# Two MLPs in a written instruction order instead of the scheduler's, on one core

## The chip, the cores and the metric

The kernel runs on one core of one Trainium2 chip. The metric is the device time of one execution, in microseconds (us). The engines are named as in the profile: PE (TensorE, matrix products), PEld (its weight loads), DVE (VectorE), ACT (ScalarE), POOL (GpSimd) and SP (SyncE, which here only issues DMAs). Each engine takes its instructions from a queue of its own, and semaphores hold an instruction until what it needs is there.

## The reference

Two layers on 256 tokens of width 2048 in float32: stick-breaking attention, then an MLP; native sparse attention (NSA), then an MLP. What the change touches is the MLP, once in each layer:

```python
def sqrelu_mlp(h, w1, w2):
    return jnp.square(jax.nn.relu(h @ w1)) @ w2
# D_MODEL = 2048, SEQ = 256, D_FF = 8192
    h = h + sqrelu_mlp(rms_norm(h, mlp_norm_g[layer]), mlp_w1[layer], mlp_w2[layer])
```

## The kernel before

**Numbers as pairs.** Every float32 operand of a product is split into two parts of a faster format, `hi` and `lo`: ACT copies it to `hi` (L142), and DVE subtracts to get `lo` (L144). A product is then three: hi by hi, lo by hi, hi by lo. The residual stream `h` stays in SBUF; `xhi`/`xlo` (tile `xs`) is the normalized and transposed input of the next projection, `yhi`/`ylo` the hidden values of an MLP.

**Chunks.** Weights arrive in chunks of 256 x 512 (512 KB), one DMA on SP each (`load`, L157), into one of five `raw` buffers; inside an MLP every sixth load goes to a buffer of its own, `raw6`. A chunk is split into one of four `hi` and four `lo` buffers and then multiplied. There are three kinds: a T chunk (`chunk_T`, L206, 24 matmuls with the weights stationary) for `x @ w1`; an N chunk (`chunk_N`, L173, 12 matmuls of 512 columns) for `y @ w2`; and an S chunk (`chunk_S`, L269), which does the same as an N chunk with 21 matmuls of 256 columns, seven products instead of eight, at the price of more work on ACT (`shi`) and DVE (`ts`, `slo`).

**The MLP.** The hidden width is done in four groups `fg` of 2048. `group1` makes 2048 hidden values in four blocks of eight T chunks; after each block ACT takes the relu, the square and `yhi`, DVE `ylo` and the sums for the S chunks (L447 to L460). `group2` multiplies them by `w2` in four column blocks: blocks 0 and 1 as N chunks, block 2 as S chunks between them (`in_S`), block 3 as S chunks between the T chunks of the next group. `add_h` and `add_S` add a finished block to `h`. In the last group of a layer block 3 is done as N chunks, and `done` is called for each block: in the first MLP it starts the next layer's input, in the second it stores the block with a DMA on SP (L1090).

**Seams.** `out_proj` ends each attention and adds its last block to `h` (L384). The input of the following MLP is made by `next_x`: two sums of squares on ACT (`junk`, L349), then for each pair of 128 columns four transposes on PE (L328), two evacuations on ACT (`xs`, L333) and two on DVE (L335). These steps lie in a list, `beside`, and `pump` takes a step from it after the two halves of each chunk.

**The order.** The code issues instructions in program order, but outside the first projection, which is written under `manual_schedule`, a scheduler reorders each engine's list by its own estimates. It may therefore put the split of a later chunk ahead of a step that waits. Memory of the pool `small`, which holds `junk`, lies ahead of the weight buffers.

## Time and profile before

| | us |
|---|---|
| median of 3 runs | 2145.69 (2145.44 to 2146.96) |
| profiled execution, its own time | 2144.79 |
| its span, first to last instruction | 2143.1 |
| first MLP, roughly | 392 to 1074 of the span |
| second MLP, roughly | 1459 to 2141 of the span |

Times in the trace are microseconds from the start of the span. A row of the order in time reads: start, duration, engine, line, operation, output tile <- input tile, shape, count, and in brackets the idle time before it and what ended it. A row by stretch gives, for each engine, busy time and number of instructions, then the granted clock of PE, the share of the DMA engines and GB/s. A matmul's duration in the trace includes a modelled end, so the distance from one start to the next is the better measure of it.

### The profile page before, as it was taken

How to read it: one execution, taken by the hardware profiler on the slowest of the kernel's cores; microseconds unless marked ns; L12 is line 12 of the kernel's file. 1: busy time of each engine (PE TensorE's matmuls, PEld its weight loads, DVE VectorE, ACT ScalarE, POOL GpSimd, SP SyncE). 2: the span in 40 equal slices, each digit the busy share in tenths (PEclk: the TensorE clock that was granted, in tenths of full speed). 3: DMA queues.
4: the chain of work that ended last, by engine and by line, in shares of the span. 5: the costliest groups of instructions: out<-in, count | busy, mean ns of one | idle time of the engine just before them, and what ended most of it. 6: DMA issues, size and time to landing. Idle time of an engine off the chain costs nothing.

```text
span 2143.1 us, 37272 instructions
## 1 busy us (share of the span) xinstructions
PE 2136.4 (100%) x14894; PEld 1973.4 (92%) x14894; DVE 1563.9 (73%) x2131; ACT 1231.6 (57%) x1653; POOL 45.2 (2%) x75
## 2 busy tenths in 40 slices
PE   9999999999999999999999999999999999999999
PEld 9999988998998999999898888889989989989998
DVE  5556556567878778778777888765678797788786
ACT  6555665555555555565555666655655555655653
POOL 0000000000000000000000111000000000000000
PEclk9999999999999999999999999999999999999999
DMA  7655556665665666665667654456656656656664
GB/s 240 210 172 177 158 180 186 186 195 188 207 202 186 205 197 203 217 197 186 194 185 217 169 145 136 149 177 187 197 170 215 205 188 213 197 189 210 204 195 149
DMA packets 260789, 406.34 MB, mean 190 GB/s; under 512 B 13188, under 2 KB 91912, under 8 KB 260616
## 3 DMA queue, kind: packets, MB, share of 16 engines
q1 hardware_dynamic: 259800, 403.52, 60.2%
q8 instruction: 116, 1.90, 0.4%
q10 hardware_dynamic: 816, 0.46, 0.1%
q14 instruction: 57, 0.47, 0.1%
HBM read 401.83 MB, written 2.10 MB: 188 GB/s over the span
## 4 chain that ended last, share of the span: by engine, by line
PE 98%; DVE 1%; DMA 0%; ACT 0%; issue 0%; POOL 0%; SPq 0%; DVEq 0%; ACTq 0%; POOLq 0%
PE acc L206 43%; PE acc L173 37%; PE att L269 12%; PE att L173 1%; PE att L328 1%; PE att L944 1%; DMA raw<-in_nsa_w_in_dram 0%; DVE lo L144 0%; PE att L655 0%; PE att L607 0%; PE att L882 0%; PE att L938 0%; PE att L884 0%; PE att L883 0%; PE att L936 0%; PE att L937 0%
## 5 line engine op out<-in xcount | busy, mean ns | idle before, releaser
L142 ACT ACTIVATE hi<-raw 128x1024 fp32r<-128x1024 f32 x639 | 676.0, 1060 | 576.1 <-PE acc L206 274.0
L144 DVE TENSOR_TENSOR lo<-raw,hi 128x1024 fp32r<-128x1024 f32 x639 | 776.6, 1222 | 252.9 <-ACT hi L142 241.3
L206 PE MATMUL acc<-xs,hi 128*128 128x256 f32 x5360 | 665.2, 277 | 0.0
L206 PEld LDWEIGHTS acc<-xs,hi 128*128 128x128 f32 x5360 | 634.4, 188 | 0.9
L206 PE MATMUL acc<-xs,lo 128*128 128x256 f32 x2680 | 359.3, 277 | 0.0
L206 PEld LDWEIGHTS acc<-xs,lo 128*128 128x128 f32 x2680 | 329.2, 188 | 0.0
L173 PE MATMUL acc<-hi,yhi 128*128 128x512 f32 x828 | 324.9, 393 | 0.0
L173 PE MATMUL acc<-hi,ylo 128*128 128x512 f32 x828 | 323.4, 391 | 0.0
L173 PE MATMUL acc<-lo,yhi 128*128 128x512 f32 x828 | 224.3, 392 | 0.0
L245 DVE TENSOR_TENSOR ts<-raw 128x512 f32<-128x512 f32 x112 | 77.4, 691 | 167.2 <-DMA raw<-in_mlp_w_dram 166.7
L142 ACT ACTIVATE hi<-ts 128x1024 fp32r<-128x1024 f32 x112 | 118.7, 1060 | 136.8 <-PE acc L173 67.8
L173 PEld LDWEIGHTS acc<-lo,yhi 128*128 128x128 f32 x828 | 154.7, 188 | 31.6
L173 PEld LDWEIGHTS acc<-hi,ylo 128*128 128x128 f32 x828 | 155.7, 188 | 29.5 <-DVE ylo L315 0.2
L173 PEld LDWEIGHTS acc<-hi,yhi 128*128 128x128 f32 x828 | 155.6, 188 | 29.5 <-ACT yhi L314 0.2
L173 PE MATMUL acc<-hi,xs 128*128 128x512 f32 x704 | 177.2, 392 | 0.0
L173 PEld LDWEIGHTS acc<-hi,xs 128*128 128x128 f32 x704 | 130.3, 188 | 26.1
L144 DVE TENSOR_TENSOR lo<-ts,hi 128x1024 fp32r<-128x1024 f32 x112 | 136.5, 1219 | 3.5 <-ACT hi L142 3.5
L247 ACT ACTIVATE shi<-raw 128x768 fp32r<-128x768 f32 x112 | 94.6, 845 | 54.8 <-PE att L269 34.5
L250 DVE TENSOR_TENSOR slo<-raw,shi 128x768 fp32r<-128x768 f32 x112 | 106.7, 953 | 4.8 <-PE att L269 4.8
L173 PE MATMUL acc<-lo,xs 128*128 128x512 f32 x352 | 97.1, 396 | 0.0
L269 PE MATMUL att<-hi,ss 128*128 128x256 f32 x672 | 94.4, 276 | 0.0
L269 PEld LDWEIGHTS att<-hi,ss 128*128 128x128 f32 x672 | 84.5, 188 | 0.0
(248 smaller groups left out, 2119.7 us busy)
## 6 DMA issues: line engine op xcount, KB each, us to landing
raw<-in_mlp_w_dram SPq DMA_DIRECT2D x512, 512.0 KB, 4.3
raw<-in_sb_w_qkv_dram SPq DMA_DIRECT2D x95, 512.0 KB, 3.9
raw<-in_nsa_w_in_dram SPq DMA_DIRECT2D x50, 512.0 KB, 3.8
raw<-in_sb_w_out_dram SPq DMA_DIRECT2D x32, 512.0 KB, 3.9
raw<-in_nsa_w_in_dram SPq DMA_DIRECT2D x64, 256.0 KB, 3.8
raw<-in_nsa_w_out_dram SPq DMA_DIRECT2D x32, 512.0 KB, 3.6
w1t<-in_nsa_cmp_w_dram SPq DMA_DIRECT2D x8, 512.0 KB, 4.0
h<-in_x_dram SPq DMA_DIRECT2D x8, 256.0 KB, 4.5
```

Of the source, the lines that this page charges most:

```text
L142: nc.scalar.activation(hi, raw, AF.Copy)
L144: nc.vector.tensor_tensor(lo, raw, hi.bitcast(F32), op=OP.subtract)
L173: mm = lambda a, b, k, t, s, e: nc.tensor.matmul(ps[t], a[:, k, t * P:(t + 1) * P], b, start=s, stop=e)
L206: nc.tensor.matmul(o, w, x[:, k0 + kk, :], start=s, stop=e, skip_group_check=True)
L245: nc.vector.tensor_tensor(ts[:, :2, :], flat[:, W:3 * W].rearrange("p (a n) -> p a n", a=2), b12, op=OP.subtract)
L247: nc.scalar.activation(hi, flat[:, :3 * W], AF.Copy)
L250: nc.vector.tensor_tensor(lo, flat[:, :3 * W], hi.bitcast(F32), op=OP.subtract)
L269: nc.tensor.matmul(ps[i], a, w, start=s, stop=e, skip_group_check=True)
L328: nc.tensor.transpose(ps[:, j * T + t * P:j * T + (t + 1) * P], h[:, t, (kp + j) * P:(kp + j + 1) * P], ident)
L944: nc.tensor.transpose(ptp[:w, j * P:(j + 1) * P], src(j), ident)
```

## The change

The MLP is issued under `manual_schedule`: PE, DVE, ACT and SP take its instructions in the order of the code. The order is written as a plan, a list of chunks with the other steps put behind chosen chunks. The evaluation of a block of hidden values is cut into four steps (relu and square; `yhi` and the sums; one half of the sums' split and `ylo`; the other half), which stand behind the third to sixth chunk that follows the block. The square is taken in place, so the tile `pre` goes; the temporary `uv` of `add_S` moves to the tile `sums`. Three extra raw buffers `more` replace `raw6`: eight in all. `junk` has one buffer instead of two. The output blocks of the second MLP are stored by a DMA on POOL's queue. Instructions keep their work; all lines after L37 move by at least one.

```diff
-        if sixth is not None and loads % 6 == 0:
-            raw = sixth.tile([P, nk, nn], F32, name="raw6", bufs=1)
+        if more is not None and loads % 8 in (2, 5, 7):
+            raw = more.tile([P, nk, nn], F32, tag="more", name="more", bufs=3)
...
-            j = small.tile([P, NB], F32, tag="junk", name="junk")
+            j = small.tile([P, NB], F32, tag="junk", name="junk", bufs=JUNK)
...
+        def relu(fb):
+            a = part["s", fb] = junk.tile([P, KB, T], F32, tag="sq", name="sq", bufs=1)
+            for j in range(0, KB, 2):
+                nc.scalar.activation(
+                    a[:, j:j + 2, :], banks["T", fb][j // 2].rearrange("p (m t) -> p m t", m=2), AF.Relu
+                )
+        def square(fb):
+            s = part["s", fb]
+            nc.scalar.activation(s, s, AF.Square)
...
+            def stages(after, j, fb):
+                put(after, j, do(relu, fb), do(square, fb))
+                for i, f in enumerate((high, low, low7)):
+                    put(after, j + 1 + i, do(f, fb))
+
+            for fg in range(NG):
+                after = {}
+                plain = sum([Ts(fg, fb) for fb in range(NF)], [])
+                if fg:
+                    put(after, 1, do(sum7, 2))
+                    put(after, 3, do(sum2, 1))
+                    Ss(fg - 1, 3, (3, 5, 10, 13, 18, 21, 26, 29), after)
+                for fb in range(NF - 1):
+                    stages(after, fb * NK + NK + 2, fb)
+                yield from merge(plain, after)
+                after = {}
+                if fg:
+                    put(after, 1, do(sum7, 3))
+                stages(after, 2, NF - 1)
+                if fg < NG - 1:
+                    plain = Ns(fg, 0) + Ns(fg, 1)
+                    Ss(fg, 2, (4, 6, 7, 9, 10, 11, 13, 14), after)
+                    put(after, 11, do(sum2, 0))
+                else:
+                    plain = Ns(fg, 0) + Ns(fg, 1) + Ns(fg, 3)
+                    put(after, 10, do(sum2, 0))
+                    Ss(fg, 2, (4, 6, 8, 10, 11, 13, 15, 17), after)
+                    put(after, 17, do(sum2, 1))
+                    put(after, 18, do(sum7, 2), *[do(done, n, (att, "att")) for n in range(3)])
+                    if last is None:
+                        put(after, 23, do(sum2, 3), do(done, 3, (att, "att")))
+                yield from merge(plain, after)
...
+        with tc.manual_schedule(engines={mybir.EngineType.PE, mybir.EngineType.DVE, mybir.EngineType.Activation,
+                                         mybir.EngineType.SP}):
+            steps = list(plan())
+            for n, c in enumerate(steps):
+                if callable(c):
+                    c()
+                    continue
...
-                nc.sync.dma_start(ov[:, :, nb * NB:(nb + 1) * NB], h[:, :, nb * NB:(nb + 1) * NB])
+                nc.gpsimd.dma_start(ov[:, :, nb * NB:(nb + 1) * NB], h[:, :, nb * NB:(nb + 1) * NB])
```

`merge` yields the chunks of `plain` in turn and after each what `after` holds for its index; `sum7` is `add_S`, `sum2` is `add_h`; `chunk1`, `chunk7` and `chunk2` call `chunk_T`, `chunk_S` and `chunk_N`.

The order on ACT at the seam into the second MLP, before: `hi` rows are splits of chunks, and the four ahead of the junk rows are those of the first four T chunks.

```order
L142 ACTIVATE hi<-raw 128x1024 x3
L142 ACTIVATE hi<-raw_15576 128x1024
L142 ACTIVATE hi<-raw 128x1024
L349 ACTIVATE junk,ssq<-h 128x512 x2
L142 ACTIVATE hi<-raw 128x1024 x2
L333 ACTIVATE xs<-att,gT 128x256 x2
L142 ACTIVATE hi<-raw 128x1024
L333 ACTIVATE xs<-att,gT 128x256 x2
```

The same place after; here the `hi<-more` row ahead of the junk rows is the split of the first T chunk, which was loaded into a `more` buffer.

```order
L143 ACTIVATE hi<-raw 128x1024
L143 ACTIVATE hi<-more 128x1024
L350 ACTIVATE junk,ssq<-h 128x512 x2
L143 ACTIVATE hi<-raw 128x1024
L334 ACTIVATE xs<-att,gT 128x256 x2
L143 ACTIVATE hi<-raw 128x1024
L334 ACTIVATE xs<-att,gT 128x256 x2
L143 ACTIVATE hi<-more 128x1024
```

The squares and the two pairs of evacuations moved three places toward the front among the splits: one split stands ahead of the squares where there were four. PE's rows there are the same in both, with the transposes after the second and the third T chunk.

The end of the first MLP on DVE, before: `lo` rows are splits of N chunks, `uv` and the `h` rows (L298) are `add_S` of the last S block, and the `lo` rows right ahead of it are of the three N chunks behind that block.

```order
L144 TENSOR_TENSOR lo<-raw_11312,hi 128x1024
L144 TENSOR_TENSOR lo<-raw,hi 128x1024 x2
L298 SCALAR_TENSOR_TENSOR h<-att,factor,h 128x512
L144 TENSOR_TENSOR lo<-raw,hi 128x1024
L294 TENSOR_TENSOR uv<-att,uv 128x256
L295 TENSOR_TENSOR uv<-att,uv 128x256
L296 TENSOR_TENSOR uv<-att,uv 128x256
L298 SCALAR_TENSOR_TENSOR h<-att,factor,h 128x512
L298 SCALAR_TENSOR_TENSOR h<-uv,factor,h 128x512 x2
L144 TENSOR_TENSOR lo<-raw,hi 128x1024 x2
```

The same place after: the one `lo<-more` row is of the only N chunk that is split between the S block and `add_S`.

```order
L145 TENSOR_TENSOR lo<-more,hi 128x1024
L295 TENSOR_TENSOR uv<-att,uv 128x256
L296 TENSOR_TENSOR uv<-att,uv 128x256
L297 TENSOR_TENSOR uv<-att,uv 128x256
L299 SCALAR_TENSOR_TENSOR h<-att,factor,h 128x512 x2
L299 SCALAR_TENSOR_TENSOR h<-uv,factor,h 128x512 x2
L145 TENSOR_TENSOR lo<-raw,hi 128x1024 x2
L336 SCALAR_TENSOR_TENSOR xs<-att,gT,xs 128x256 x4
```

The whole of `add_S` moved ahead of two or three splits. On ACT at that place, the squares and the evacuations for the next layer's input stand, before, behind the splits of chunks that PE reaches later:

```order
L142 ACTIVATE hi<-raw 128x1024 x3
L293 ACTIVATE uv<-att 128x256
L142 ACTIVATE hi<-raw 128x1024
L349 ACTIVATE junk,ssq<-h 128x512
L142 ACTIVATE hi<-raw 128x1024
L333 ACTIVATE xs<-att,gT 128x256 x4
L349 ACTIVATE junk,ssq<-h 128x512
L142 ACTIVATE hi<-raw 128x1024 x2
L333 ACTIVATE xs<-att,gT 128x256 x4
```

After, each group of evacuations stands right behind the split of the chunk around whose `lo` matmuls PE makes the transposes:

```order
L143 ACTIVATE hi<-more 128x1024
L294 ACTIVATE uv<-att 128x256
L143 ACTIVATE hi<-raw 128x1024
L350 ACTIVATE junk,ssq<-h 128x512 x2
L143 ACTIVATE hi<-raw 128x1024
L334 ACTIVATE xs<-att,gT 128x256 x4
L143 ACTIVATE hi<-more 128x1024
L350 ACTIVATE junk,ssq<-h 128x512 x2
L143 ACTIVATE hi<-raw 128x1024
L334 ACTIVATE xs<-att,gT 128x256 x4
L143 ACTIVATE hi<-more 128x1024
```

So an evacuation moved from a place four splits later to the place right behind the split of its own chunk; on PE the first two of the three pairs of transposes in the MLP's last chunks stand one N chunk later, and the third pair follows the second at once.

## The prediction

> **What bounds the kernel now.** I read the page's engine table first, then the busy time by stretch (cut at the borders of the two MLPs), then who waits for whom on TensorE, then the order in time at the places where the new order differs.

> ```profile
> span 2143.1 us, 37272 instructions
> PE 2136.4 (100%) x14894; PEld 1973.4 (92%) x14894; DVE 1563.9 (73%) x2131; ACT 1231.6 (57%) x1653; POOL 45.2 (2%) x75
> PE 98%; DVE 1%; DMA 0%; ACT 0%; issue 0%; POOL 0%; SPq 0%; DVEq 0%; ACTq 0%; POOLq 0%
> ```
> ```profile
> 391.00:1060.00 669.00, 669.00 (x5074) 636.00 (x5073) 520.81 (x647) 381.08 (x413) 0.70 (x1) 1.00 0.62 198
> 1090.00:1458.80 368.80, 367.78 (x1931) 308.93 (x1930) 275.13 (x537) 226.95 (x483) 24.30 (x18) 1.00 0.58 168
> 1473.00:2120.00 647.00, 647.00 (x4906) 615.30 (x4905) 504.51 (x622) 366.36 (x387) 0.00 (x0) 1.00 0.63 199
> 2120.00:2143.10 23.10, 19.12 (x101) 16.28 (x99) 10.30 (x15) 3.97 (x5) 0.00 (x0) 1.00 0.16 57
> ```
> ```profile
> PE att L515 <- POOL ident masks.py:199: 1.6, 1, 1.6
> PE att L789 <- DVE hs L784: 0.5, 1, 0.5
> ```

> TensorE is the bound, at clock 1.00, and in both MLPs it has no idle time: 669.00 of 669.00 and 647.00 of 647.00. Its waits of a whole run are led by 1.6 us, at the very start. So there is nothing in the MLPs that a better order could save: the change can only keep TensorE fed as well, or worse. The profiled execution took 2144.8 (span 2143.1 and 1.7 around it); the median of the runs is 0.9 above it.

> **The change, part by part.** TensorE's own list stays the same matmuls; in six groups one S chunk stands one T chunk later, which costs nothing while no operand is late.

> *Square in place, four steps.* The same four ACT and six DVE instructions per block; only their places move. Over the first MLP ACT is busy 381 of 669 us and DVE 521, both in the shadow of TensorE, so their durations cost 0 as long as splits keep ahead. In the steady groups they do: relu is placed after the third chunk of the next block and waits for the last of the old one, so three split chunks, of 2.8 us each (below), stand ready for TensorE. 0.

> *8 raw buffers.* Loads run further ahead, past DVE's waits for weights:

> ```profile
> DVE ts L245 <- DMA raw<-in_mlp_w_dram: 166.7, 81, 4.2
> ```

> That is much, but it is DVE's idle time, and TensorE waited for none of it. Gain 0; no loss either, DMA is busy 0.63.

> *The written order at the seam into each MLP.* This is where I see the price. Into the second MLP the trace of before runs like this:

> ```profile
> 1458.14 1.06 ACT L142 ACTIVATE hi<-raw 128x1024 fp32r<-128x1024 f32 x1 [1.61 <-PE acc L173]
> 1458.85 2.05 PE L206 MATMUL acc<-xs,hi 128*128 128x256 f32 x16
> 1459.54 0.63 ACT L349 ACTIVATE junk<-h 128x512 f32<-128x512 f32 x1 [0.34 <-DVE h L384]
> ...
> 1460.98 1.06 ACT L142 ACTIVATE hi<-raw 128x1024 fp32r<-128x1024 f32 x1
> ...
> 1461.67 2.05 PE L206 MATMUL acc<-xs,hi 128*128 128x256 f32 x16
> ...
> 1464.50 0.60 PE L328 MATMUL att<-ident,h 128*128 128x128 f32 x4
> 1464.85 2.07 PE L206 MATMUL acc<-xs,hi 128*128 128x256 f32 x16
> ...
> 1465.14 0.84 ACT L333 ACTIVATE xs<-att,gT 128x256 fp32r<-128x256 f32 x2 [0.27 <-PE att L328]
> ```

> A T chunk lasts 2.82 (1458.85 to 1461.67). At 1458.85 ACT has split the first four chunks; the `hi` at 1460.98 is already that of the fifth. So the squares (junk), which wait for the last block of `h`, and the evacuations (xs), which wait for transposes, delay splits that are not urgent. In the new order ACT has one split, then the two squares, then the second split, xs, the third split, xs, the fourth. Nothing is in hand. TensorE's order is unchanged, so:
> - Second chunk: its `hi` can't start before 1460.98, ends 1462.04, and TensorE wants it at 1461.67: with 0.1 for the handover 0.5 late.
> - Third chunk: the transposes ahead of it start at 1464.50 and are followed 0.35 later by the chunk. Now that chunk's `hi` stands behind xs on ACT: 0.64 until xs starts, 0.84 for the two, 1.06 for `hi`, less 0.35: 2.2 late. Handover (0.1) and the 0.1 by which ACT's instructions overlap cancel.
> - Fourth chunk: the same, 2.2. After it ACT has no more of these and needs 1.06 per 2.82: it recovers.

> The sum is 4.9 per seam. The seam into the first MLP has the same rows, so twice: 9.8. DVE's `lo` (1.2) follows each `hi` and is needed only after sixteen matmuls (1.88, 1464.85 to 1466.73): covered. The page of before has this very chain once, in its first stage, where the order is also written out: transposes, xs, `hi` behind xs, and TensorE waits:

> ```profile
> 5.68 0.84 ACT L333 ACTIVATE xs<-att,gT 128x256 fp32r<-128x256 f32 x2 [2.59 <-PE att L328]
> 6.41 1.17 ACT L527 ACTIVATE hi<-raw 128x512 fp32r<-128x512 f32 x2
> 7.09 0.41 PE L534 MATMUL acc<-xs,hi 128*128 128x256 f32 x1 [0.17 <-ACT hi L527]
> ```

> There the first half `hi` (0.6) lets TensorE start 1.41 after xs began; a full one makes it 1.9, and 0.64 + 1.9 - 0.35 is again 2.2. [...]

> *The end of an MLP.* Here the sums of the last S block (uv, then four times h, on DVE) come one N chunk after that block, where before three splits were in hand:

> ```profile
> 2122.44 0.28 PE L269 MATMUL att<-lo,yhi 128*128 128x256 f32 x1
> ...
> 2124.20 0.42 DVE L294 TENSOR_TENSOR uv<-att,uv 128x256 f32<-128x256 f32 x1
> ...
> 2127.30 1.22 DVE L144 TENSOR_TENSOR lo<-raw,hi 128x1024 fp32r<-128x1024 f32 x1
> ```

> From the first uv to the next `lo` are 3.10 with three of the four h in between; the fourth adds 0.67. S ends at 2122.55; the chain can start at 2122.64, its `lo` at 2126.4 and end at 2127.6. TensorE wants it one N chunk (2.72) and eight matmuls of the next (1.82) after S, at 2127.1. 0.6 late with the handover, in each MLP. In the first MLP the next layer's xs follow in the written order too, a pair on either side of a chunk's `lo` matmuls:

> ```profile
> 1059.81 0.60 PE L328 MATMUL att<-ident,h 128*128 128x128 f32 x4
> 1061.03 1.62 ACT L333 ACTIVATE xs<-att,gT 128x256 fp32r<-128x256 f32 x4
> 1061.18 0.60 PE L328 MATMUL att<-ident,h 128*128 128x128 f32 x4
> ```

> Before, these four ran after a split four chunks ahead. Now the split of the very next chunk stands behind them: the second pair is bound to the second transposes, so 2.2 late again, once. The second time twelve transposes stand ahead of the next chunk instead of four (about 1.2 instead of 0.35): 1.3 late. First MLP's end 0.6 + 2.2 + 1.3 = 4.1, second 0.6.

> *Junk with one buffer, and NSA's order.* Between 1090 and 1458.8 TensorE idles 1.0, so a gain ends at 1.0. For a loss the nearest row is its wait of 0.5 for hs; six such would be 3. I take 0, since the scheduler places these itself and the rows there stay nearly the same; ends -1 and +3.

> *The three output blocks on POOL's queue.*

> ```profile
> out_dram<-h SPq DMA_DIRECT2D x3, 512.0 KB, 5.9
> 2139.16 0.88 DVE L394 SCALAR_TENSOR_TENSOR h<-acc,factor,h 128x256 f32<-128x256 f32 x2 [0.55 <-PE acc L181]
> ```

> On SP the waits for h end the weight loads' queue; POOL has nothing behind them. The third block is ready at 2127.4, lands by 2133.3 at 5.9, and the last sums start at 2139.16: POOL may be 5.9 slower before it shows. No row has a DMA issued by POOL: ends 0 and +3; 0 taken, for that margin.

> Sum: 9.8 + 4.1 + 0.6 = 14.5. Against the profiled execution 2144.8 + 14.5 = 2159.3, against the median 2160.2. I forecast 2160, slower by 0.7%. Each of the six large stalls may be off by 0.3 (handover and overlap), NSA by -1 to +3, POOL by 0 to 3: 2157 to 2167 if the mechanism is right.

> **The rivals.**
> - *No loss at the seams* (not slower). It needs splits to be in hand when xs waits, or xs not to hold the split. For it: ACT is only 57% busy, and in the steady groups I find no wait. Against: the order of ACT's rows, and 7.09 above. It decides at the third chunk: if its `hi` starts before xs there, 10 to 13 us of the sum fall. 2146 (2144 to 2149).
> - *More: DVE falls behind in the S stretches.*

> ```profile
> 650.00:700.00 50.00, 50.00 (x285) 43.74 (x284) 44.93 (x59) 28.95 (x30) 0.00 (x0) 1.00 0.61 201
> 2113.38 1.41 DVE L386 SCALAR_TENSOR_TENSOR h<-acc,factor,h 128x512 f32<-128x512 f32 x2
> ```

> DVE is 90% busy there, and in a fixed order h (1.41) stands between an S split and the next `lo`. By hand I find some 1 to 2 us in hand at the closest. If that is wrong, 1.4 per group in eight groups adds 11: 2171.
> - *More: the clock.* All rows show clock 1.00. Were the granted clock to halve for one chunk after each of the six stalls of over 1 us, each would cost another 2.8: 17 more, 2177. [...]
> - *Faster.* TensorE is idle 4.0 in the last 23.1 us and 1.0 in NSA. If one-queue effects there went away, at most about 2: 2144, which is still within 0.2%.

> **How the numbers follow.** Chances: forecast 0.73, DVE behind 0.10, clock 0.03, no loss 0.12, faster 0.02. The range reaches up to the DVE case (2171) and down to where half of the sum would be hidden (7 of 14.5: 2153, and 3 for the bounds below); it leaves out no loss, faster and clock, 0.17 together: 2150 to 2172. About 0.2% is what a measurement of this kernel can tell from no change: slower 0.73 + 0.10 + 0.03 = 0.86, same 0.13 (no loss, and half of the faster case), faster 0.01.

> **What would show it.** TensorE's waits should now name ACT `hi` (L143 there) after the first three chunks of each MLP, some 0.5, 2.2 and 2.2, and twice near the end of the first; DVE `lo` 0.6 once near each end. Busy TensorE between the seams should stay at 100%. The steps are wrong if those waits are missing, or if DVE or a DMA is named inside the groups. The forecast falls if the fourth split is found in ACT's queue before the transposes have run.

## The result and the profile after

The changed kernel takes 2163.55 us (median of 6 runs, 2162.51 to 2168.14) where the kernel before, run beside it, takes 2145.66 (6 runs). The ratio is 1.0087, with a 95% interval from 1.0074 to 1.0100: 17.9 us slower. The forecast was 2160, within 2150 to 2172. The profiled execution took 2162.7, its span is 2161.0, so the two spans differ by the same 17.9, and the trace can be used to find them.

Two lines of the page of after; the second is the engine table, busy time and share:

```profile
span 2161.0 us, 37053 instructions
PE 2141.2 (99%) x14894; PEld 1975.2 (91%) x14894; DVE 1578.0 (73%) x2131; ACT 1211.6 (56%) x1653; POOL 45.6 (2%) x78
```

TensorE has the same 14894 matmuls but is busy 4.8 longer than before (2136.4), and idle 19.8 instead of 6.7. So there are two things to find: 13.1 us more of waiting, and 4.8 us more in which TensorE counts as busy.

The busy time by stretch of after, cut around the two starts of an MLP (397.50 and 1475.00), the groups (410.00 and 1489.00) and the end of the first MLP (1066.00). The columns are as before: PE, PEld, DVE, ACT, POOL, then TensorE's granted clock, the share of the DMA engines and GB/s.

```profile
397.50:410.00 12.50, 8.75 (x60) 8.28 (x59) 6.59 (x11) 7.46 (x10) 0.70 (x1) 0.86 0.44 128
410.00:1066.00 656.00, 656.00 (x4966) 623.25 (x4964) 517.50 (x632) 359.32 (x392) 0.00 (x0) 1.00 0.64 198
1066.00:1096.00 30.00, 25.51 (x162) 22.18 (x162) 20.65 (x31) 19.36 (x38) 4.73 (x13) 1.00 0.44 130
1475.00:1489.00 14.00, 10.25 (x73) 9.78 (x73) 7.50 (x12) 7.35 (x10) 0.70 (x1) 0.88 0.48 136
1489.00:2144.00 655.00, 655.00 (x4958) 622.45 (x4957) 516.62 (x631) 359.92 (x390) 1.63 (x2) 1.00 0.63 198
```

In the groups TensorE has no idle time at all, 656.00 of 656.00 and 655.00 of 655.00. Nearly all of the loss sits in three short stretches: both seams and the end of the first MLP. And in the two seams the clock column is not 1.00.

Who waits for whom on TensorE, after (total, times, longest):

```profile
PE acc L207 <- ACT hi L143: 7.7, 5, 1.9
PE acc L174 <- ACT hi L143: 2.9, 2, 1.9
PE att L584 <- POOL ident masks.py:199: 1.6, 1, 1.6
PE acc L174 <- DVE lo L145: 1.1, 2, 0.6
PE acc L207 <- ACT xs L334: 1.1, 1, 1.1
PE att L887 <- DVE a L878: 1.0, 1, 1.0
```

The first row is the seams (T chunks, L207), the second the end of the first MLP (N chunks, L174), the fourth the ends of the two MLPs, and the fifth the border from the first MLP to NSA. The third row was there before. The order in time at the second seam shows the queue behind them:

```profile
1471.90 1.04 ACT L143 ACTIVATE hi<-raw 128x1024 fp32r<-128x1024 f32 x1
1473.00 2.11 PE L207 MATMUL acc<-xs,hi 128*128 128x256 f32 x16 [0.19 <-ACT hi L143]
1475.85 0.60 PE L329 MATMUL att<-ident,h 128*128 128x128 f32 x4
1476.49 0.84 ACT L334 ACTIVATE xs<-att,gT 128x256 fp32r<-128x256 f32 x2 [3.54 <-PE att L329]
1477.22 1.05 ACT L143 ACTIVATE hi<-raw 128x1024 fp32r<-128x1024 f32 x1
1478.33 2.10 PE L207 MATMUL acc<-xs,hi 128*128 128x256 f32 x16 [1.87 <-ACT hi L143]
1481.82 0.84 ACT L334 ACTIVATE xs<-att,gT 128x256 fp32r<-128x256 f32 x2 [3.54 <-PE att L329]
1482.55 1.05 ACT L143 ACTIVATE hi<-more 128x1024 fp32r<-128x1024 f32 x1
1483.65 2.63 PE L207 MATMUL acc<-xs,hi 128*128 128x256 f32 x16 [1.87 <-ACT hi L143]
```

ACT idles 3.54 ahead of each pair of xs, because xs waits for the transposes; the split for the very next chunk stands behind it, and TensorE then idles 1.87 for that split. This is the chain that was forecast. What was not forecast is in the last row: sixteen matmuls that take 2.10 after the first stall take 2.63 after the second. The same view by stretch, cut where the clock changes (first seam, then second):

```profile
403.05:406.47 3.42, 1.54 (x13) 1.31 (x12) 1.81 (x3) 2.75 (x5) 0.00 (x0) 1.00 0.38 135
406.47:409.88 3.41, 3.41 (x18) 3.41 (x17) 2.56 (x6) 2.93 (x3) 0.70 (x1) 0.50 0.57 164
409.88:413.29 3.41, 3.41 (x32) 3.41 (x31) 2.84 (x4) 1.06 (x1) 0.00 (x0) 1.00 0.90 288
1481.67:1485.08 3.41, 1.54 (x13) 1.43 (x13) 2.33 (x4) 3.27 (x5) 0.00 (x0) 1.00 0.27 102
1485.08:1488.49 3.41, 3.41 (x19) 3.41 (x18) 2.56 (x6) 2.30 (x3) 0.70 (x1) 0.50 0.70 194
```

After each seam's second stall TensorE runs 3.41 us at clock 0.50: 18 or 19 matmuls where the next stretch of the same length has 32. TensorE is "busy" all that time, which is why the waits alone do not explain the 17.9. Each of the two stretches costs about half its length, 1.6 to 1.7, so together they make 3.3 of the 4.8. Part of the rest is the way of counting: the last matmul ahead of a stall counts as busy up to its modelled end, so that a stall of 1.87 idle costs 2.1 from start to start.

### The profile page after: what moved, and what is told of

It reads as the page before. It is cut to its first block, busy times and chain, and to the rows that moved or that the text cites. A ratio compares the mean times of both kernels' runs of the same rounds, so it can differ in the third digit from the quotient of the medians.

```text
span 2161.0 us, 37053 instructions
## 1 busy us (share of the span) xinstructions
PE 2141.2 (99%) x14894; PEld 1975.2 (91%) x14894; DVE 1578.0 (73%) x2131; ACT 1211.6 (56%) x1653; POOL 45.6 (2%) x78
## 5 line engine op out<-in xcount | busy, mean ns | idle before, releaser
L145 DVE TENSOR_TENSOR lo<-raw,hi 128x1024 fp32r<-128x1024 f32 x495 | 601.6, 1221 | 262.2 <-ACT hi L143 252.4
L143 ACT ACTIVATE hi<-raw 128x1024 fp32r<-128x1024 f32 x495 | 520.3, 1055 | 343.1 <-PE acc L207 133.6
L207 PE MATMUL acc<-xs,hi 128*128 128x256 f32 x5360 | 666.7, 277 | 8.7 <-ACT hi L143 7.7
L207 PEld LDWEIGHTS acc<-xs,hi 128*128 128x128 f32 x5360 | 635.8, 188 | 11.2 <-ACT hi L143 8.8
L207 PE MATMUL acc<-xs,lo 128*128 128x256 f32 x2680 | 360.4, 277 | 0.0
L207 PEld LDWEIGHTS acc<-xs,lo 128*128 128x128 f32 x2680 | 330.6, 189 | 0.0
L174 PE MATMUL acc<-hi,yhi 128*128 128x512 f32 x828 | 324.5, 392 | 2.9 <-ACT hi L143 2.9
L174 PE MATMUL acc<-hi,ylo 128*128 128x512 f32 x828 | 323.0, 390 | 0.0
L145 DVE TENSOR_TENSOR lo<-more,hi 128x1024 fp32r<-128x1024 f32 x144 | 175.8, 1221 | 72.0 <-ACT hi L143 71.4
L174 PE MATMUL acc<-lo,yhi 128*128 128x512 f32 x828 | 224.3, 392 | 1.1 <-DVE lo L145 1.1
L143 ACT ACTIVATE hi<-ts 128x1024 fp32r<-128x1024 f32 x112 | 118.6, 1059 | 170.0 <-DVE ts L250 168.8
L143 ACT ACTIVATE hi<-more 128x1024 fp32r<-128x1024 f32 x144 | 151.6, 1053 | 70.4 <-PE acc L207 32.6
L174 PEld LDWEIGHTS acc<-hi,yhi 128*128 128x128 f32 x828 | 155.5, 188 | 32.9 <-ACT hi L143 3.3
L174 PEld LDWEIGHTS acc<-lo,yhi 128*128 128x128 f32 x828 | 154.5, 188 | 33.6 <-DVE lo L145 2.0
L174 PEld LDWEIGHTS acc<-hi,ylo 128*128 128x128 f32 x828 | 155.5, 188 | 29.6 <-DVE ylo L316 0.2
L174 PE MATMUL acc<-hi,xs 128*128 128x512 f32 x704 | 177.8, 392 | 0.0
L174 PEld LDWEIGHTS acc<-hi,xs 128*128 128x128 f32 x704 | 130.0, 188 | 26.0
L248 ACT ACTIVATE shi<-raw 128x768 fp32r<-128x768 f32 x64 | 53.9, 841 | 97.5 <-PE att L270 97.5
L174 PE MATMUL acc<-lo,xs 128*128 128x512 f32 x352 | 96.7, 395 | 0.0
## 6 DMA issues: line engine op xcount, KB each, us to landing
raw<-in_mlp_w_dram SPq DMA_DIRECT2D x320, 512.0 KB, 4.2
more<-in_mlp_w_dram SPq DMA_DIRECT2D x192, 512.0 KB, 4.1
raw<-in_sb_w_qkv_dram SPq DMA_DIRECT2D x95, 512.0 KB, 4.4
raw<-in_nsa_w_in_dram SPq DMA_DIRECT2D x50, 512.0 KB, 4.1
raw<-in_sb_w_out_dram SPq DMA_DIRECT2D x32, 512.0 KB, 3.8
raw<-in_nsa_w_out_dram SPq DMA_DIRECT2D x32, 512.0 KB, 3.6
w1t<-in_nsa_cmp_w_dram SPq DMA_DIRECT2D x8, 512.0 KB, 4.0
```

What stands on the lines that cost most here:

```text
L143: nc.scalar.activation(hi, raw, AF.Copy)
L145: nc.vector.tensor_tensor(lo, raw, hi.bitcast(F32), op=OP.subtract)
L174: mm = lambda a, b, k, t, s, e: nc.tensor.matmul(ps[t], a[:, k, t * P:(t + 1) * P], b, start=s, stop=e)
L207: nc.tensor.matmul(o, w, x[:, k0 + kk, :], start=s, stop=e, skip_group_check=True)
L248: nc.scalar.activation(hi, flat[:, :3 * W], AF.Copy)
```

## The experiments

Two theories had to be told apart. Mine, with the profile in hand: the fixed order on ACT and DVE makes all of the loss, through stalls at the seams and the ends, and the half clock follows from the stalls. The rivals: other parts of the change (four steps, buffers, one junk, POOL's queue) cost part of it, or the clock has another cause.

**Four splits ahead of the seam.** In the changed kernel the splits of an MLP's first four chunks are issued before its first chunk:

```diff
-        banks, part = {}, {}
+        banks, part, ready = {}, {}, []
...
+            if (fg, fb, i) == (0, 0, 0):
+                ready.extend(load_split(w1, c * KC, KC, 0, NB, o=(FAR, FAR)) for c in range(4))
+            src = ready.pop(0) if ready else w1
-            chunk_T(banks["T", fb], w1, i * KC, fg * D + fb * NB, i == 0, i == NK - 1)
+            chunk_T(banks["T", fb], src, i * KC, fg * D + fb * NB, i == 0, i == NK - 1)
```

> The changed kernel, with the splits (hi, lo) of the first four chunks of each MLP issued ahead of its first chunk, so that on ACT they stand before the two squares (junk) and the two pairs of evacuations (xs). Nothing else differs. Order theory: TensorE's waits at the two seams go (0.25 + 2.12 + 2.15 = 4.5 each), and with them the two stretches of 3.41 us at half clock that follow them (1.7 each): 2163.6 - 2 x 4.5 - 2 x 1.7 = 2151, granted clock 1.000 up to the end. Rival, the clock halves for another reason than these stalls: 2154.5, clock 0.998 still. Rival, the wait only moves (the fifth split now stands behind both pairs of xs, by my sum 0.8 us in time): a wait of about 2 at the fifth chunk of each MLP, 2155.

Measured: 2151.92 (2151.50 to 2153.98, 5 runs), ratio to the kernel before 1.0032 (1.0019 to 1.0044); in the profiled run the clock is 1.000 up to the end (0.999 in one of the five, 2153.98; the stalls at the end of the first MLP are still there). The order in time at its first seam:

```profile
397.56 2.07 PE L207 MATMUL acc<-xs,hi 128*128 128x256 f32 x16
397.85 0.84 ACT L334 ACTIVATE xs<-att,gT 128x256 fp32r<-128x256 f32 x2 [4.33 <-PE att L329]
400.74 2.08 PE L207 MATMUL acc<-xs,hi 128*128 128x256 f32 x16
401.02 0.84 ACT L334 ACTIVATE xs<-att,gT 128x256 fp32r<-128x256 f32 x2 [2.34 <-PE att L329]
401.75 1.06 ACT L143 ACTIVATE hi<-raw 128x1024 fp32r<-128x1024 f32 x1
403.56 1.98 PE L207 MATMUL acc<-xs,hi 128*128 128x256 f32 x16
```

ACT still idles for the transposes, 4.33 and 2.34, but now nothing urgent stands behind them: the split that starts at 401.75 is that of the fifth chunk, it ends at 402.8, and TensorE starts this chunk at 403.56. Stalls and half clock are gone together. The wait did not move to a later chunk: from 385 to 420 and from 1455 to 1500 TensorE waits for nothing.

**Splits ahead at the end.** The last N block of each MLP takes its splits two chunks ahead:

```diff
+        coming, ahead = [], [2]
...
+            src = w2
+            if (fg, nb) == (NG - 1, 3) and i >= 2:
+                while ahead[0] < min(i + 3, NK):
+                    coming.append(load_split(w2, fg * KD + ahead[0] * KC, KC, nb * NB, NB, o=(FAR, FAR)))
+                    ahead[0] += 1
+                src = coming.pop(0)
...
-            chunk_N(banks["N", nb], w2, fg * KD + i * KC, nb * NB, first, end, yhi, ylo, koff=fg * KD,
+            chunk_N(banks["N", nb], src, fg * KD + i * KC, nb * NB, first, end, yhi, ylo, koff=fg * KD,
```

> The changed kernel, with the splits of the last N block of each MLP issued two chunks ahead, so that two are in hand when the sums of the last S block (uv, h) and the next layer's squares and xs come. Order theory: TensorE's waits for lo (0.6 at each end) and for hi and xs near the end of the first MLP (1.9 + 1.0 and 1.1 at its border to NSA) go, some 4 to 5 in all: 2159. The seams stay as they are, with their two stretches at half clock: clock 0.998. Rival, the work behind the last S block is simply more than ACT and DVE can hide there and the waits move into the next stage: 2162 to 2164.

Measured: 2159.22 (2154.65 to 2162.36, 5 runs), ratio 1.0062 (1.0048 to 1.0076). The waits for lo, for the N chunks' hi and for xs have left the list; 7.7 for the T chunks' hi stay, to the tenth. The scatter is wide, and the clock, 0.997 to 0.999 over the five runs, shows one reason. The stalls at its two seams are alike. Here are the slots of 3.41 us in which the second stall of each seam falls, and the ones behind them:

```profile
403.41:406.82 3.41, 1.54 (x15) 1.30 (x13) 0.96 (x3) 1.90 (x4) 0.00 (x0) 1.00 0.58 154
406.82:410.23 3.41, 3.41 (x29) 3.41 (x30) 2.56 (x5) 3.41 (x4) 0.70 (x1) 1.00 0.30 66
1478.61:1482.02 3.41, 1.54 (x14) 1.30 (x13) 1.83 (x3) 2.76 (x5) 0.00 (x0) 1.00 0.38 133
1482.02:1485.43 3.41, 3.41 (x19) 3.41 (x18) 2.56 (x6) 2.91 (x3) 0.70 (x1) 0.50 0.54 159
```

The same stall, with the same 1.54 us of busy time left in its slot, was followed by clock 1.00 once and by 0.50 once. That the time came out at the 2159 expected is in part luck: the profiled run has one stretch at half clock less (1.7), and it has a late start (1.6) and a stretch of slower matmuls (2.3 in 60 us), of which the last section tells.

**Both.** The two edits together:

> Both of these edits of the changed kernel together. Order theory: the price of the fixed order is all in these four places, and what is left is the time of the kernel before: 2163.6 - 12.4 - 4.5 = 2146.7, with 0.5 either way, clock 1.000. Rival, part of the loss lies elsewhere (the four steps, the one junk buffer, the output blocks on POOL's queue): 2149 or more with TensorE's waits named at such places.

Measured: 2144.28 (2143.50 to 2145.84, 11 runs), ratio 0.9992 (0.9983 to 1.0001), clock 1.000. That is the time of the kernel before, and 19 us less than the changed one. None of TensorE's longest waits of the changed kernel inside the MLPs is left.

**The scheduler again.** The changed kernel with all its parts, but without the fixed order:

```diff
-        with tc.manual_schedule(engines={mybir.EngineType.PE, mybir.EngineType.DVE, mybir.EngineType.Activation,
-                                         mybir.EngineType.SP}):
+        if True:
```

> The changed kernel without the one statement that makes the MLPs' order fixed; four steps, square in place, eight raw buffers, one junk buffer and POOL's queue for the output stay, and the scheduler places all of it. Order theory: 2146, within 0.2% of the kernel before, no waits at the seams, clock 1.000. Rival, the other parts cost part of the 17.9: clearly above 2150, by as much as they cost.

Measured: 2144.01 (2143.18 to 2145.16, 11 runs), ratio 0.9992 (0.9984 to 1.0001), no wait of TensorE between 380 and 1100. So the four steps, the square in place, the eight raw buffers, the one junk buffer and POOL's queue together cost nothing: the fixed order is the whole loss. ACT's own order in time at the first seam of this kernel:

```profile
393.82 1.06 ACT L143 ACTIVATE hi<-raw 128x1024 fp32r<-128x1024 f32 x1 [0.26 <-PE acc L207]
396.54 1.06 ACT L143 ACTIVATE hi<-more 128x1024 fp32r<-128x1024 f32 x1 [1.66 <-PE acc L207]
397.89 0.84 ACT L334 ACTIVATE xs<-att,gT 128x256 fp32r<-128x256 f32 x2 [0.29 <-PE att L329]
399.72 1.06 ACT L143 ACTIVATE hi<-raw 128x1024 fp32r<-128x1024 f32 x1 [0.99 <-PE acc L207]
```

Here ACT idles 0.29 ahead of xs, not 3.54 as above: the scheduler fills the time ahead of it with splits of later chunks.

**Three splits instead of four.** The first edit with `range(3)`, so that one stall per seam is left:

> The changed kernel with the splits of the first three chunks of each MLP ahead of its first chunk, where the first experiment had four. Order theory: the fourth chunk's split alone stands behind a pair of xs, so each seam keeps one stall of 2.1 instead of two and a small one: 2151.9 + 2 x 2.1 = 2156.2 without the clock. Clock theories: if one stall of about 1.9 inside one slot of 3.41 us is enough to halve the clock in the next slot, a run has 0 to 2 stretches of 3.41 us at half clock, 1.7 each, by how the slots happen to lie: 2156 to 2160. If it takes two such stalls in a row, none: 2156, clock 1.000 up to the end in each run.

Measured: 2156.94 (2156.42 to 2157.42, 5 runs), ratio 1.0050 (1.0036 to 1.0063); the clock is 1.000 in three of the runs and 0.999 in two. That is 5.0 more than with four splits, but it was measured on another chip, where the kernel before took 2146.48 instead of 2145.64. Against the kernel before beside each it is 4.2 more, as two stalls of 2.1 make. At the seams no half clock followed in the profiled run; at the second one the stall lay across the border of two slots, and the emptier of the two still had 1.77 us of busy time. After a single stall of 1.9 at the end of the first MLP half clock did follow:

```profile
1476.14:1479.55 3.41, 1.77 (x16) 1.53 (x14) 1.11 (x3) 1.60 (x3) 0.00 (x0) 1.00 0.00 0
1479.55:1482.96 3.41, 3.18 (x27) 3.18 (x28) 2.75 (x5) 3.41 (x5) 0.48 (x1) 1.00 0.26 40
...
1066.56:1069.97 3.41, 1.53 (x10) 1.12 (x9) 2.81 (x5) 2.85 (x7) 0.00 (x0) 1.00 0.14 50
1069.97:1073.38 3.41, 3.41 (x10) 2.63 (x9) 1.39 (x2) 1.22 (x3) 0.00 (x0) 0.50 0.00 0
```

So in this run one such stall was enough.

**A probe of the clock.** The version with both edits, with a repeated `hi` in 30 blocks (there are 30 that the condition selects, not 31 as I wrote), to give stalls of many sizes at many places in the slots:

```diff
         nc.scalar.activation(hi, raw, AF.Copy)
+        for w in delay:
+            nc.scalar.activation(hi[:, :, :w], raw[:, :, :w], AF.Copy)
+        delay.clear()
...
+            if i == 5 and (fg or fb):
+                us = 8.6 + 0.13 * len(probes)
...
```

Measured: 2383.61, one run; the 30 stalls came out at 3.6 to 8.6 us, longer than I had meant, so none of them is below 3.4. Their parts in a slot still cover a range, 1.59 to 2.82 us in those below. The slots around four of them:

```profile
454.97:458.38 3.41, 1.82 (x17) 1.62 (x15) 0.00 (x0) 3.31 (x4) 0.00 (x0) 1.00 0.00 0
458.38:461.79 3.41, 0.87 (x7) 0.87 (x8) 0.89 (x1) 3.35 (x5) 0.00 (x0) 1.00 0.00 0
461.79:465.20 3.41, 3.41 (x18) 3.41 (x18) 3.41 (x4) 2.98 (x4) 0.00 (x0) 0.50 0.55 150
...
608.57:611.98 3.41, 1.08 (x10) 0.89 (x8) 0.00 (x0) 3.31 (x4) 0.00 (x0) 1.00 0.00 0
611.98:615.39 3.41, 1.81 (x8) 1.81 (x9) 1.83 (x2) 2.25 (x3) 0.00 (x0) 0.50 0.00 0
615.39:618.80 3.41, 3.41 (x18) 3.41 (x17) 2.75 (x5) 2.12 (x3) 0.00 (x0) 0.50 0.70 172
618.80:622.21 3.41, 3.41 (x32) 3.41 (x31) 3.41 (x4) 2.86 (x3) 0.00 (x0) 1.00 0.38 138
...
966.97:970.38 3.41, 1.54 (x14) 1.34 (x12) 0.00 (x0) 3.31 (x4) 0.00 (x0) 1.00 0.00 0
970.38:973.79 3.41, 0.59 (x5) 0.59 (x6) 0.61 (x1) 3.31 (x5) 0.00 (x0) 1.00 0.00 0
973.79:977.20 3.41, 3.41 (x19) 3.41 (x18) 3.08 (x6) 1.33 (x3) 0.00 (x0) 0.50 0.44 120
...
1069.37:1072.78 3.41, 1.36 (x12) 1.15 (x10) 0.00 (x0) 3.31 (x4) 0.00 (x0) 1.00 0.00 0
1072.78:1076.19 3.41, 1.17 (x5) 1.17 (x6) 1.19 (x2) 2.86 (x4) 0.00 (x0) 0.50 0.00 0
```

In these rows a slot with 1.82 or 1.54 of busy time left the clock alone; one with 0.59, 0.87, 1.08 or 1.36 was followed by half clock in the next. The slot at half clock with 1.81 busy was followed by another at 0.50, the one behind it with 3.41 busy by clock 1.00 (618.80).

In the changed kernel the two stretches at half clock start 1078.61 apart (406.47 and 1485.08), which is 316 times 3.413: they lie on one grid. Over all slots of that grid in its trace, half clock set in twice while TensorE had matmuls left, behind the two slots with 1.54 busy; behind the next emptiest ones, with 1.61 and 2.01, the clock stayed 1.00:

```profile
1072.06:1075.48 3.42, 2.01 (x9) 1.66 (x10) 2.10 (x3) 3.39 (x8) 0.00 (x0) 1.00 0.01 2
1075.48:1078.89 3.41, 3.41 (x19) 2.84 (x18) 1.23 (x1) 0.36 (x2) 0.00 (x0) 1.00 0.16 32
...
1474.84:1478.25 3.41, 1.61 (x15) 1.38 (x13) 0.88 (x2) 1.76 (x3) 0.00 (x0) 1.00 0.57 154
1478.25:1481.67 3.42, 3.34 (x28) 3.21 (x28) 1.23 (x1) 0.03 (x1) 0.00 (x0) 1.00 0.29 54
```

All rows shown here fit the theory of slots: half clock behind 0.59 to 1.36 in the probe, 1.53 in the run with three splits, 1.54 twice in the changed kernel and once with the end mended; clock 1.00 behind 1.54 once with the end mended and once in the probe, and behind 1.61, 1.77, 1.82 and 2.01. So 1.54 busy, or 1.87 idle, went either way, and between 1.36 and 1.53 there is no row. Busy time here includes the modelled end of a matmul, so these figures are known in this way of counting only. Of the rivals, the slot idle from end to end falls with these rows; two stalls in a row fall with the single stall of the run with three splits, since the probe has no stall short enough to test them.

**The output blocks on SP's queue.** The version with both edits, with the one line undone:

```diff
-                nc.gpsimd.dma_start(ov[:, :, nb * NB:(nb + 1) * NB], h[:, :, nb * NB:(nb + 1) * NB])
+                nc.sync.dma_start(ov[:, :, nb * NB:(nb + 1) * NB], h[:, :, nb * NB:(nb + 1) * NB])
```

> The version with both edits (2144.3), with the three finished output blocks issued by SP again instead of POOL; nothing else differs. My term for POOL's queue was 0, with ends 0 and +3: then this kernel takes the same, 2144 to 2145, and the same as the next run of the version with both edits. Rival, POOL's queue costs time at the end: this one is faster by as much, up to 3. Rival, on SP the waits for h hold up the last weight loads, which POOL avoided: slower, and TensorE waits for a DMA or DVE in the last 30 us.

> The version with both edits once more, beside the one with SP's queue and the kernel before on one chip: 2144 to 2146, within 0.2% of the kernel before; a gain, if there is one, is 0.5 to 1.5 us, and two sets of runs together should tell whether it is more than the scatter of either kernel.

Measured on one chip: 2148.86 on SP (2146.30 to 2149.50, 11 runs, ratio to before 1.0008, 0.9999 to 1.0017), 2144.27 on POOL (2143.78 to 2145.76, 11 runs, ratio 0.9991, 0.9982 to 1.0000). The two sets do not overlap. SP's queue near the end, first on SP with TensorE's wait, then with POOL:

```profile
2102.40 0.37 SPq L158 DMA_DIRECT2D raw<-in_mlp_w_dram  x1
2102.82 23.62 SPq L1169 DMA_DIRECT2D out_dram<-h  x3
2126.54 0.42 SPq L158 DMA_DIRECT2D more<-in_mlp_w_dram  x1
...
PE acc L174 <- ACT hi L143: 3.0, 1, 3.0
```
```profile
2102.24 0.37 SPq L158 DMA_DIRECT2D raw<-in_mlp_w_dram  x1
2103.38 0.37 SPq L158 DMA_DIRECT2D more<-in_mlp_w_dram  x1
2106.84 2.64 SPq L158 DMA_DIRECT2D raw<-in_mlp_w_dram  x2
```

In the fixed order the stores stand on SP ahead of the last three loads and wait for h; the loads go out at 2126.5 instead of 2103.4, and TensorE waits 3.0 for a split whose weights are late (ACT idles 10.35 for that DMA). The second rival holds. The rest of the 4.6 between the medians is not traced: six of the eleven runs on SP show clock 0.999 where all eleven on POOL show 1.000, so a slot at half clock behind the wait is likely in those. POOL's queue thus avoids a loss that the stores would make on SP at this place in the written order; writing them behind the last loads was not tried. In the kernel before, the scheduler had left one load behind the second store (2114.81, the load at 2116.81) and none behind the third (2127.41).

The version with both edits, and the changed kernel under the scheduler, are clearly better than the changed kernel. Against the kernel before they are 0.08% to 0.09% faster in all three sets, with intervals that reach 1.0000 or 1.0001: a gain of 1.4 to 2.4 us, by the medians, is likely but not shown.

## Why the prediction was right, and where it was not

The start of each numbered matmul in after, less that of the same number in before, gives the loss by step (worked out from the two traces):

| step | forecast | measured |
|---|---|---|
| stalls, first seam | 4.9 | 4.4 |
| stalls, second seam | 4.9 | 4.7 |
| end of the first MLP | 4.1 | 4.4 |
| end of the second MLP | 0.6 | 0.9 |
| groups | 0 | -0.4 |
| NSA, with its border | 0 (-1 to +3) | 1.3 - 1.0 |
| POOL's stores | 0 (0 to +3) | 0.0 |
| half clock | not in the sum | 1.6 + 1.7 |
| start, and ahead of the first MLP | not in the sum | 0.5 |
| sum (rounded after adding) | 14.5 | 18.0 |

- *The seams.* Right in place, cause and size. The stalls are 1.9 by the list of waits and cost 2.1 each from start to start; I had 2.2. That a split does not pass the xs that waits ahead of it on ACT is what the rows of after show: 3.54 of idle ahead of xs, and the split right behind it. The early one, 0.5 in the sum, is 0.2 at the second seam and not in the list at the first. The experiment with four splits takes all of it away.
- *The end of an MLP.* DVE lo is named twice with 0.6, as forecast; hi twice near the end of the first, 1.9 and 1.0 for my 2.2 and 1.3. The experiment with splits ahead at the end takes these waits away.
- *Groups, steps, buffers.* No loss, as forecast (0.2 less in each MLP). A block has five ACT instructions, two of them relu, not the four that I counted; since ACT is off TensorE's path there, that changes nothing. The rival of DVE falling behind has no row anywhere.
- *NSA.* The 0 came out by luck, from two things that nearly cancel: a wait of 1.1 for xs at the border, which I had not seen (four xs stand behind a split there), and a stretch of slower matmuls that the kernel before had in its profiled run (258 in 30 us, against 267 in the same stage of this one; more below).
- *POOL.* The term of 0 against the kernel before is right. My reason (nothing stands behind the stores on POOL) is, too. That the stores end the loads' queue on SP was not quite so even before (one load stood behind the second), and that they would cost 4.6 there in the new order I did not ask.
- *The clock.* Here the prediction failed. It gave the half clock 3 in 100, an estimate that no row of before could bear out: they all show clock 1.00, but TensorE's longest wait there is 1.6, at the very start. Measured, a stall of 1.87 that left 45% of a slot of 3.41 busy (1.54) was followed by clock 0.50 at both seams. The price was wrong too: no run shows a whole chunk lost to the clock behind each stall, the 2.8 of the rival; it was 1.65 for a slot, and behind two of the six stalls, not all. The 3.3 us are nearly the whole difference of 3.5 between sum and measurement. The range held because they are small, not because it allowed for them.

Two of the changed kernel's six runs took 2167 and 2168. They have no trace, and their clock is 0.998 like that of the profiled run, so more stretches at half clock do not explain them; I leave their extra 4 us open.

## What to carry to other kernels

In the fixed order a wait became a wait of all that stood behind it: ACT idled 3.54 ahead of each pair of xs with the next chunk's split behind it, and three stores on SP held loads back until 2126.5 that went out from 2103.4 on without them. So before one writes the order out, list for each waiting instruction what is behind it, on ACT and DVE and on the DMA queue, and put enough finished work ahead of it (here four splits at a seam, two at an end). When a tensor engine that was never idle gets stalls, look in the trace for two prices: the stall itself, 2.1 here, and a stretch of 3.41 us at clock 0.50 behind it, 1.6 to 1.7 here. In the changed kernel two of six stalls had the second one, both with 1.54 us of a slot left busy; slots with 1.61 or more left busy had none in the rows shown.

## What else the runs showed

*Matmuls that are 4% slower at clock 1.00.* In 60 us of the first MLP, with TensorE busy throughout, the kernel with the end mended issued 511 matmuls where the version with both edits issued 531 in the same stretch:

```profile
420.00:480.00 60.00, 60.00 (x511) 60.00 (x511) 36.30 (x39) 33.77 (x37) 0.00 (x0) 1.00 0.61 184
```
```profile
420.00:480.00 60.00, 60.00 (x531) 59.96 (x530) 37.38 (x38) 31.95 (x34) 0.00 (x0) 1.00 0.65 203
```

For each matmul that is 117 ns instead of 113, and the 20 that are missing are 2.3 us. The kernel before has such a stretch of some 30 us from 1086, with no stall ahead of it that the list of waits names (258 matmuls, where the changed kernel has 267). What sets it off was not found.

*The start.* In the traces of before and after, TensorE's clock record begins, with full clock, 7.2 and 7.1 us after the first instruction, and ahead of that the matmuls come at about half speed: the same four transposes take 1.11 there and 0.60 behind it.

```profile
4.53 1.11 PE L328 MATMUL att<-ident,h 128*128 128x128 f32 x4
10.12 0.60 PE L328 MATMUL att<-ident,h 128*128 128x128 f32 x4
```

In the run with the end mended 17 matmuls ran between 7.0 and 10.8 where the version with both edits had 31; the 14 that are missing are 1.6 us at 113 ns. With the slower stretches this may make part of the scatter of one to two microseconds between runs of one kernel.
